# Modulation weights in 1 MB tiles, tokens by feature, and norms from a product with ones, in a hybrid decoder step

## The chip, the cores and the metric

The kernel runs on one core of one Trainium2 chip. Its engines are TensorE (PE; its weight loads are shown as PEld), VectorE (DVE), ScalarE (ACT), GpSimd (POOL) and SyncE (SP); 16 DMA engines move data between HBM and SBUF. The metric is the device time of one execution in microseconds, taken as the median of several runs. A profile is one further execution, recorded by the hardware profiler.

## What is computed

One decoder layer for 512 prompt tokens and 32 sampled tokens (8 sequences of 4), with 1024 features. Cut to what matters here:

```python
def ada_modulation(c, w_ada, b_ada):                  # w_ada: (1024, 6 * 1024)
    mod = (jax.nn.silu(c) @ w_ada + b_ada).reshape(c.shape[0], 6, 1024)
    return [mod[:, None, i] for i in range(6)]

def rms_norm(x, gain):
    return x * lax.rsqrt(jnp.mean(x * x, axis=-1, keepdims=True) + EPS) * gain

def decoder_layer(x, c, ...):
    sh_m, sc_m, gt_m, sh_f, sc_f, gt_f = ada_modulation(c, w_ada, b_ada)
    h = rms_norm(x, g_norm_mix) * (1 + sc_m) + sh_m
    u, q, k, v, g_a, g_b = jnp.split(h @ w_in, cuts, axis=-1)
    a = pool_mixer(u, ...) @ w_branch_pool
    o = attend(q, k, v) @ w_branch_attn               # prompt: causal; sampled: 3 best of 16 cached blocks
    x = x + gt_m * ((sigmoid(g_a) * a + sigmoid(g_b) * o) @ w_out)
    h2 = rms_norm(x, g_norm_ffn) * (1 + sc_f) + sh_f
    f_gate, f_val = jnp.split(h2 @ w_up, 2, axis=-1)
    return x + gt_f * ((silu(causal_dwconv(f_gate)) * f_val) @ w_down)
```

There are 9 condition vectors c: one for the prompt, eight for the sampled sequences. The sampled tokens read paged caches of K and V, 64 MB each as they are gathered here.

## The kernel before

**Work and stages.** All 544 tokens (512 and 32) go through the dense layers together. A weight piece of 128 x 1024 floats (a granule, 0.5 MB) is split into a high and a low part (`split`), and each product is three fp32r products (`mm3`). The stages are: h from x, then q, k and v, the prompt's attention with u between, the gates, the branches, w_out, up and down. Beside this dense stream runs the sampled stream: it gathers K in 64 tiles of 1 MB (`kstep`), chooses blocks, gathers V in 64 tiles, and multiplies the other modulation columns. A planner in the kernel deals the two streams out on TensorE by a running estimate of TensorE's time (`PE.now`) and of when a tile has landed. From there each engine works its queue off in order.

**The start.** `load_constants` (L282) loads x by token, two tiles of 256 tokens and one of 32 (`xin`). `norms` (L513) squares and sums each token's row on ScalarE, forms 1/sqrt(mean + eps) for each token, and spreads the 544 values over all partitions as rows (`rows`) by products with the identity. `turned` turns one feature block of 128 to 128 x 512 with four transposes on TensorE, `normed` multiplies it by the rows.

`quarter(i)` (L549) does two of the eight feature blocks: it multiplies the conditions by the shift and scale columns of these blocks, in two tiles of w_ada (kind `m0`, eight in all), turns and adds the bias (`modT`), forms the gain (`gsm`), and makes h for the sampled (`put_sample_h`) and the prompt's tokens (`put_prompt_h`) in high and low parts. The q projection follows the quarters: granule g of q takes h of quarter g, and quarter g + 1 is dealt out between its products. A `pair` or `st` tile holds a q granule; the sampled tokens' q is a product of the raw tile with `h1s`.

**What sets the order around the change.** SP's queue holds, in the program's order: cT, the constants, x, the `m0` tiles with one or two granules between, the page table (`ptb`), then granules, constants and gains. A transfer there waits for what its memory held before, and all behind it wait too. The tiles `m0` with numbers 2 to 4 have memory of their own (`m`), which `ptb` later uses again; so `ptb` waits until TensorE has read the fifth of them. `page_indices` (L299) makes the row numbers on VectorE, behind the third quarter's work there, and the first gather of K on GpSimd's queue waits for them. Each `m0` tile is loaded by two transfers, one for the shift and one for the scale columns, in runs of 256 floats (1 KB); the tiles of the other columns come in runs of 8 KB (`mod`) or 4 KB (`one`).

Of the kernel before, what the change touches and what calls it, by code (L numbers as in the profile page):

```python
# [74 lines left out]
def body(ctx, tc, I, O):  # L75
# [198 lines left out]
    xin = [consts.tile([128, 2, D], F32, name=uid("xin")) for _ in range(2)] + [consts.tile([NS, D], F32, name="xsin")]  # L274
# [7 lines left out]
    def load_constants():  # L282
        in_order(nc.sync.dma_start(cst[:, 0:CFIRST], I["const"][:, 0:CFIRST]))
        for i in range(2):
            in_order(nc.sync.dma_start(xin[i], I["x"][i * 256:(i + 1) * 256].rearrange("(t p) d -> p t d", p=128)))
        in_order(nc.sync.dma_start(xin[2], I["x"][S:T]))
# [31 lines left out]
    class Stream:  # L318
# [7 lines left out]
        def pump(self):  # L326
            while self.issued < len(self.items) and self.issued < self.at + NKV:
# [16 lines left out]
                elif kind == "m0":  # L344
                    rows = I["w_ada"][a[1] * 512:(a[1] + 1) * 512].rearrange("(k p) c -> p k c", p=128)
                    for v in range(2):
                        c0 = v * D + a[0] * 256
                        in_order(nc.sync.dma_start(kt.rearrange("p (k v c) -> p k v c", k=4, v=2)[:, :, v], rows[:, :, c0:c0 + 256]))
# [9 lines left out]
                elif kind == "mod":  # L358
                    pin(nc.gpsimd.dma_start(kt, I["w_ada"][a[1] * 128:(a[1] + 1) * 128, a[0] * 2048:(a[0] + 1) * 2048]))
                elif kind == "one":  # L360
                    pin(nc.gpsimd.dma_start(kt.rearrange("p (k c) -> p k c", k=2),
                                            I["w_ada"][a[1] * 256:(a[1] + 1) * 256, a[0] * D:(a[0] + 1) * D].rearrange("(k p) c -> p k c", p=128)))
                else:
                    pin(nc.gpsimd.dma_start(kt.rearrange("p (g c) -> p g c", g=2), I["wpack"][a:a + 2].rearrange("g p c -> p g c")))
# [139 lines left out]
    def dense1():  # L504
        hh, hl = [slot([128, T], F32R) for _ in range(8)], [slot([128, T], F32R) for _ in range(8)]
        ssx = consts.tile([128, 8], F32, name="ssx")
# [6 lines left out]
        def norms():  # L513

            rstd = consts.tile([128, 8], F32, name="rstd")
            for t in range(5):
                n, xt = (128, xin[t // 2][:, t % 2]) if t < 4 else (NS, xin[2])
                junk = wsh.next()
                act(junk[:n], xt[:n], AF.Square, accum_out=ssx[:n, t:t + 1])
                if t % 2 == 1 or t == 4:  # L520
                    c = slice(t // 2 * 2, t + 1)
                    V.tensor_scalar(rstd[:n, c], ssx[:n, c], 1.0 / D, EPS, op0=OP.mult, op1=OP.add)
                    act(rstd[:n, c], rstd[:n, c], AF.Sqrt)
                    V.reciprocal(rstd[:n, c], rstd[:n, c])
# [3 lines left out]
            PE.matmul(prs, rstd[:NS, 4:5].to_broadcast([NS, 128]), ident[:NS, :NS], start=True, stop=True)  # L528
            act(rows[:, 0:S], pr)
            act(rows[:, S:T], prs)  # L530

        def normed_sampled():
            prs = mm([128, 8, NS], "hT")
            for f in range(8):
                PE.transpose(prs[:, f], xin[2][:, f * 128:(f + 1) * 128], ident[:NS, :NS])
            return prs
# [1001 lines left out]
```

## Time and profile before

| what | value |
|---|---|
| time, median of 3 runs | 1002.61 us (1002.35 to 1004.32) |
| the profiled execution: time, span | 1004.91 us, 1003.0 us |
| TensorE busy | 955.2 us, 95% of the span |
| VectorE, ScalarE, GpSimd busy | 46%, 33%, 14% |
| moved by DMA | 236.62 MB |
| mean granted clock of TensorE | 0.98 |

How to read it: busy shares are means over stages with different limits, so a stage is looked at by itself, in a stretch of the timeline. Timeline rows merge equal instructions that follow each other: start, duration of the whole row, the instruction with out<-in by the program's names, a count, and in brackets the idle time before it and what ended it. An fp32 product shows as two records, an fp32r product as one. L163 and L167 are the lines of the helpers through which all products and transposes go, so tile names tell them apart: `hT` transposes and spread rows, `mod` modulation, `qkv` the projections, `qk` the cached K.

### The profile page before, as it was taken

How to read it: one execution, taken by the hardware profiler on the slowest of the kernel's cores; microseconds unless marked ns; L12 is line 12 of the kernel's file. 1: busy time of each engine (PE TensorE's matmuls, PEld its weight loads, DVE VectorE, ACT ScalarE, POOL GpSimd, SP SyncE). 2: the span in 40 equal slices, each digit the busy share in tenths (PEclk: the TensorE clock that was granted, in tenths of full speed). 3: DMA queues.
4: the chain of work that ended last, by engine and by line, in shares of the span. 5: the costliest groups of instructions: out<-in, count | busy, mean ns of one | idle time of the engine just before them, and what ended most of it. 6: DMA issues, size and time to landing. Idle time of an engine off the chain costs nothing.

```text
span 1003.0 us, 20225 instructions
## 1 busy us (share of the span) xinstructions
PE 955.2 (95%) x8674; PEld 809.6 (81%) x8674; DVE 465.9 (46%) x1071; ACT 328.8 (33%) x662; POOL 143.9 (14%) x157
## 2 busy tenths in 40 slices
PE   5979997999989999999999979999999999999998
PEld 3557775655579987777686779999989999999997
DVE  2572444656643332212384486554423545445455
ACT  5251425523422244111232354322233323123320
POOL 0043232133333332232200000000000000000000
PEclk9998999899999999999999989999999999999999
DMA  9799999499999996999956303222322222222222
GB/s 303 256 383 420 416 403 415 161 423 412 387 374 391 412 390 256 422 417 420 406 192 250 109 25 106 85 85 86 98 71 85 85 84 90 97 89 93 85 85 68
DMA packets 56266, 236.62 MB, mean 236 GB/s; under 512 B 5361, under 2 KB 17553, under 8 KB 38769
## 3 DMA queue, kind: packets, MB, share of 16 engines
q0 software_dynamic: 22848, 155.20, 38.1%
q1 hardware_dynamic: 33328, 80.13, 23.5%
q8 instruction: 68, 1.11, 0.4%
q14 instruction: 22, 0.17, 0.1%
HBM read 230.37 MB, written 4.94 MB: 235 GB/s over the span
## 4 chain that ended last, share of the span: by engine, by line
PE 86%; DMA 5%; ACT 4%; DVE 3%; issue 1%; POOL 0%; SPq 0%; DVEq 0%; ACTq 0%
PE up L163 26%; PE dn L163 13%; PE gate L163 10%; PE qkv L163 7%; PE pv L163 5%; PE qk L163 5%; PE wo L163 4%; PE mod L163 3%; PE O L163 2%; PE A L163 2%; DMA kv<-in_kT,kidx 2%; ACT spots L183 2%; ACT s L183 1%; DMA kv<-in_v,vidx 1%; PE u L163 1%; DVE s L180 1%
## 5 line engine op out<-in xcount | busy, mean ns | idle before, releaser
L180 DVE TENSOR_TENSOR lo<-st,hi 128x1024 fp32r<-128x1024 f32 x108 | 132.2, 1224 | 249.0 <-ACT hi L183 245.4
L163 PE MATMUL up<-s,hi 128*128 128x272 f32 x1408 | 234.6, 288 | 0.1
L183 ACT ACTIVATE hi<-st 128x1024 fp32r<-128x1024 f32 x108 | 114.4, 1059 | 342.1 <-PE up L163 115.5
L163 PEld LDWEIGHTS up<-s,hi 128*128 128x128 f32 x1408 | 199.1, 188 | 0.4 <-ACT hi L183 0.4
L163 PE MATMUL up<-s,lo 128*128 128x272 f32 x704 | 146.3, 288 | 0.5 <-DVE lo L180 0.5
L163 PE MATMUL dn<-s,hi 128*128 128x272 f32 x704 | 117.7, 289 | 0.0
L163 PEld LDWEIGHTS up<-s,lo 128*128 128x128 f32 x704 | 111.1, 188 | 0.7 <-DVE lo L180 0.7
L163 PEld LDWEIGHTS dn<-s,hi 128*128 128x128 f32 x704 | 98.9, 188 | 3.4 <-issue 2.5
L338 POOL DMA_INDIRECT kv<-in_kT,kidx x64 | 65.8, 1028 | 169.0 <-PE qk L163 104.7
L163 PE MATMUL gate<-s,hi 128*128 128x272 f32 x512 | 89.7, 296 | 0.0
L342 POOL DMA_INDIRECT kv<-in_v,vidx x64 | 63.7, 995 | 147.8 <-PE pv L163 116.7
L163 PEld LDWEIGHTS gate<-s,hi 128*128 128x128 f32 x512 | 72.5, 189 | 11.5 <-issue 10.4
L183 ACT ACTIVATE s<-s 128x544 f32<-128x544 f32 (+4 forms) x74 | 46.7, 644 | 81.1 <-DVE s L1269 37.5
L163 PE MATMUL dn<-s,lo 128*128 128x272 f32 x352 | 72.8, 288 | 0.0
L163 PE MATMUL qkv<-hi,s 128*128 128x512 f32 x192 | 70.2, 421 | 2.3 <-ACT s L183 2.0
L163 PE MATMUL qk<-kv,qblk 128*32 128x128 f32 x2048 | 65.2, 277 | 6.1 <-DVE qblk L632 1.9
L163 PEld LDWEIGHTS qk<-kv,qblk 128*32 128x32 f32 x2048 | 55.1, 111 | 15.0 <-issue 8.9
L163 PE MATMUL pv<-kv,spots 128*32 128x512 f32 x512 | 63.3, 605 | 0.4 <-DMA kv<-in_v,vidx 0.4
L180 DVE TENSOR_TENSOR s<-s,s 128x544 fp32r<-128x544 f32 (+4 forms) x78 | 53.6, 700 | 14.0 <-ACT s L183 13.6
L163 PEld LDWEIGHTS qkv<-hi,s 128*128 128x128 f32 x192 | 37.0, 193 | 23.0 <-issue 12.2
L163 PEld LDWEIGHTS dn<-s,lo 128*128 128x128 f32 x352 | 55.2, 188 | 0.0
L163 PE MATMUL gate<-s,lo 128*128 128x272 f32 x256 | 53.0, 288 | 0.0
(217 smaller groups left out, 1183.7 us busy)
## 6 DMA issues: line engine op xcount, KB each, us to landing
st<-in_wpack SPq DMA_DIRECT2D x108, 512.0 KB, 3.4
kv<-in_w_ada POOLq DMA_DIRECT2D x16, 1024.0 KB
kv<-in_w_ada SPq DMA_DIRECT2D x10, 512.0 KB, 10.9
kv<-in_wpack POOLq DMA_DIRECT2D x4, 1024.0 KB
pair<-in_wpack SPq DMA_DIRECT2D x6, 512.0 KB, 14.2
m<-in_w_ada SPq DMA_DIRECT2D x6, 512.0 KB, 4.7
xin<-in_x SPq DMA_DIRECT2D x2, 1024.0 KB, 7.5
s<-in_x SPq DMA_DIRECT2D x8, 256.0 KB, 6.4
```

The lines of the kernel that those rows point to most:

```text
L163: return self.add(nc.tensor.matmul(out, lhsT, rhs, **kw))
L180: V.tensor_tensor(out, a, b, op)
L183: A.activation(out, x, func, **kw)
L338: pin(nc.gpsimd.indirect_dma_start(out=kt, out_offset=None, in_=krows, in_offset=bass.IndirectOffsetOnAxis(ap=kidx[:, i:i + 1], axis=0)))
L342: pin(nc.gpsimd.indirect_dma_start(out=kt, out_offset=None, in_=vrows, in_offset=bass.IndirectOffsetOnAxis(ap=vidx[:, i:i + 1], axis=0)))
```

## The change

Three layouts change, made from the inputs before the kernel starts. The modulation weights come as 24 tiles of 128 x 2048 floats, each contiguous, 8 KB for a partition; every tile is one transfer. x comes a second time by feature, as four tiles of 128 x (2 x 544) (`xT`); x by token is still read later for the residual. The transposes of x, `turned` and `normed_sampled`, go away. The norms are found from x by feature: each block is squared on ScalarE, two squares are added on VectorE, and a product with ones sums over the 128 features of a block into every partition, for both halves of the tokens; mean, eps, square root and reciprocal then run on 128 x 272 instead of one column a token block. The products of one `m0` tile are bound into a run (`PE.begin`, `PE.end`).

```diff
+    xT = consts.tile([128, KD, T], F32, name="xT")
+    ones = consts.tile([128, 1], F32, name="ones")
+    V.memset(ones, 1.0)
...
-        for i in range(2):
-            in_order(nc.sync.dma_start(xin[i], I["x"][i * 256:(i + 1) * 256].rearrange("(t p) d -> p t d", p=128)))
-        in_order(nc.sync.dma_start(xin[2], I["x"][S:T]))
+        for i in range(4):
+            in_order(nc.sync.dma_start(xT[:, 2 * i:2 * i + 2], I["xT"][i].rearrange("p (f c) -> p f c", f=2)))
...
                 elif kind == "m0":
-                    rows = I["w_ada"][a[1] * 512:(a[1] + 1) * 512].rearrange("(k p) c -> p k c", p=128)
-                    for v in range(2):
-                        c0 = v * D + a[0] * 256
-                        in_order(nc.sync.dma_start(kt.rearrange("p (k v c) -> p k v c", k=4, v=2)[:, :, v], rows[:, :, c0:c0 + 256]))
+                    in_order(nc.sync.dma_start(kt, I["wada"][j]))
...
                 elif kind == "mod":
-                    pin(nc.gpsimd.dma_start(kt, I["w_ada"][a[1] * 128:(a[1] + 1) * 128, a[0] * 2048:(a[0] + 1) * 2048]))
+                    pin(nc.gpsimd.dma_start(kt, I["wada"][8 + a[1]]))
                 elif kind == "one":
-                    pin(nc.gpsimd.dma_start(kt.rearrange("p (k c) -> p k c", k=2),
-                                            I["w_ada"][a[1] * 256:(a[1] + 1) * 256, a[0] * D:(a[0] + 1) * D].rearrange("(k p) c -> p k c", p=128)))
+                    pin(nc.gpsimd.dma_start(kt, I["wada"][16 + 4 * (a[0] - 4) + a[1]]))
...
         def norms():
-            rstd = consts.tile([128, 8], F32, name="rstd")
-            for t in range(5):
-                n, xt = (128, xin[t // 2][:, t % 2]) if t < 4 else (NS, xin[2])
-                junk = wsh.next()
-                act(junk[:n], xt[:n], AF.Square, accum_out=ssx[:n, t:t + 1])
...
-            pr, prs = mm([128, S], "hT"), mm([128, NS], "hT")
-            for t in range(4):
-                PE.matmul(pr[:, t * 128:(t + 1) * 128], rstd[:, t:t + 1].to_broadcast([128, 128]), ident, start=True, stop=True)
...
+            pr = [mm([128, HALF], "hT") for _ in range(2)]
+            for i in range(4):
+                sq = [slot([128, T]) for _ in range(2)]
+                for j in range(2):
+                    act(sq[j], xT[:, 2 * i + j], AF.Square)
+                tt(sq[0], sq[0], sq[1], OP.add)
+                for o, (a, b) in zip(pr, BOTH):
+                    PE.matmul(o, ones.to_broadcast([128, 128]), sq[0][:, a:b], start=i == 0, stop=i == 3)
+            for o, (a, b) in zip(pr, BOTH):
+                V.tensor_scalar(rows[:, a:b], o, 1.0 / D, EPS, op0=OP.mult, op1=OP.add)
+                act(rows[:, a:b], rows[:, a:b], AF.Sqrt)
+                V.reciprocal(rows[:, a:b], rows[:, a:b])
...
-        def turned(f):
-            ps = mm([128, S], "hT")
-            for t in range(4):
-                PE.transpose(ps[:, t * 128:(t + 1) * 128], xin[t // 2][:, t % 2, f * 128:(f + 1) * 128], ident)
-            return ps
-        def normed(ps):
+        def normed(f):
             x = slot([128, S])
-            tt(x, ps, rows[:, 0:S], OP.mult)
+            tt(x, xT[:, f, 0:S], rows[:, 0:S], OP.mult)
             return x
...
             if i == 0:
-                raw = [turned(0), turned(1)]
-                prs = normed_sampled()
                 norms()
...
+            xT2 = [normed(f0), normed(f0 + 1)]
             ps = mm([128, 256], "mod")
             for a in range(2):
                 st = KV.get("m0").rearrange("p (k v c) -> p k v c", k=4, v=2)
+                PE.begin()
                 for kk in range(4):
                     for v in range(2):
                         j = 2 * (kk % 2) + v
                         PE.matmul(ps[32 * j:32 * j + 32], csT[:, 4 * a + kk], st[:, kk, v],
                                          start=a == 0 and kk < 2, stop=a == 1 and kk >= 2)
+                PE.end()
                 KV.next()
...
-            if i:
-                xT = [normed(turned(f0))]
...
+def pack_modulation(w):
+    w = w.reshape(KD, 128, 6, D)
+    tiles = [w[4 * h:4 * h + 4, :, 0:2, c * 256:(c + 1) * 256].transpose(1, 0, 2, 3) for c in range(4) for h in range(2)]
+    tiles += [w[k, :, 2:4] for k in range(KD)]
+    tiles += [w[2 * k:2 * k + 2, :, v].transpose(1, 0, 2) for v in (4, 5) for k in range(4)]
+    return np.stack([t.reshape(128, 2048) for t in tiles])
```

The change moves instructions at three places. The first is SP's queue from the first `m0` tile on. In brackets stand the semaphores a transfer waits for: `DMAHW` names are those of earlier transfers on the queue, the others are engines. Before:

```order
L348 DMA kv<-in_w_ada 128x4x256 [waits DMAHW1_49]
L220 DMA pair_100<-in_wpack 128x1024 [waits DMAHW2_49,PE_49,Pool_49]
L348 DMA m_102<-in_w_ada 128x4x256 [waits DMAHW3_49]
...
L348 DMA kv<-in_w_ada 128x4x256 [waits DMAHW3_49]
L220 DMA pair_112<-in_wpack 128x1024 [waits DMAHW4_49,DVE_49,PE_49]
L348 DMA kv<-in_w_ada 128x4x256 [waits DMAHW5_49]
...
L289 DMA ptb<-in_page_table 128x256 [waits DMAHW1_49,PE_49]
```

In the changed kernel, the same stretch of SP's queue:

```order
L347 DMA kv<-in_wada 128x2048 [waits DMAHW0_49]
L220 DMA pair_99<-in_wpack 128x1024 [waits DMAHW1_49]
L347 DMA m_101<-in_wada 128x2048 [waits DMAHW2_49]
...
L347 DMA kv<-in_wada 128x2048 [waits DMAHW6_49]
L220 DMA pair_107<-in_wpack 128x1024 [waits DVE_49,DMAHW7_49,PE_49,Activation_49]
L347 DMA kv<-in_wada 128x2048 [waits DMAHW0_49]
L347 DMA kv<-in_wada 128x2048 [waits DMAHW1_49]
L291 DMA ptb<-in_page_table 128x256 [waits DMAHW3_49,DMAHW5_49,DMAHW2_49,PE_49]
```

Eight `m0` transfers stand where sixteen stood. By the values they wait for, the first pair waited for the last product that spreads the norms, and now waits for no engine. The second waited for the first pair to be split and multiplied by `h1s`; it now waits for TensorE's last product with ones and for earlier work of VectorE and ScalarE. The page table still waits for the product that reads the fifth `m0` tile.

The second place is VectorE's queue from the norms to the first gain; `s` are working tiles, `xsT` the normed sampled tokens. Before:

```order
L522 TENSOR_SCALAR rstd<-ssx 128x2
L522 TENSOR_SCALAR rstd<-ssx 32x1
L524 RECIPROCAL rstd<-rstd 128x2
L524 RECIPROCAL rstd<-rstd 32x1
L180 TENSOR_TENSOR s_181<-hT_136,s_133 128x512
L180 TENSOR_TENSOR xsT<-hT_146,s_133 128x256
L180 TENSOR_TENSOR s_183<-hT_141,s_133 128x512
L180 TENSOR_TENSOR modT<-mod_224,par 128x2x18
L581 SCALAR_TENSOR_TENSOR gsm<-modT,par 128x18
```

In the changed kernel:

```order
L180 TENSOR_TENSOR s_153<-s_153,s_154 128x544
L521 TENSOR_SCALAR s_127<-hT_130 128x272
L521 TENSOR_SCALAR s_127<-hT_131 128x272
L523 RECIPROCAL s_127<-s_127 128x272 x2
L180 TENSOR_TENSOR xsT<-xT,s_127 128x256
L180 TENSOR_TENSOR s_168<-xT,s_127 128x512
L180 TENSOR_TENSOR s_170<-xT,s_127 128x512
L180 TENSOR_TENSOR modT<-mod_209,par 128x2x18
L560 SCALAR_TENSOR_TENSOR gsm<-modT,par 128x18
```

The bias of the first quarter (`modT`) stands behind two reciprocals of 272 columns instead of three of one or two columns.

The third place is TensorE's queue at the second quarter, between the first q products; `m` is the tile of modulation weights. Before:

```order
L163 MATMUL qkv_243<-hi,s_114 128x512
L163 MATMUL mod_253<-m_102,csT 32x256
L163 MATMUL qkv_243<-lo,s_114 128x512
L163 MATMUL qkv_244<-hi,s_114 128x512
L163 MATMUL qkv_244<-lo,s_114 128x512
L163 MATMUL mod_253<-m_102,csT 32x256 x7
...
L163 MATMUL mod_253<-m_102,csT 32x256
L167 MATMUL hT_280<-cst,xin_84 128x128 x2
L167 MATMUL hT_280<-cst,xin_85 128x128 x2
L163 MATMUL qkv_246<-hi,s_114 128x512
```

In the changed kernel:

```order
L163 MATMUL qkv_228<-hi,s_109 128x512
L163 MATMUL qkv_228<-lo,s_109 128x512
L163 MATMUL mod_242<-m_101,csT 32x256 x8
L163 MATMUL qkv_229<-hi,s_109 128x512
L163 MATMUL qkv_229<-lo,s_109 128x512
L163 MATMUL qkv_228<-hi,s_117 128x512
L163 MATMUL qkv_229<-hi,s_117 128x512
L163 MATMUL mod_242<-m_101,csT 32x256 x8
```

The transposes of x are gone, and the eight products of a tile stand together. Of the six tiles dealt out among the q products, four stood divided before; two do now (the fifth tile, one and seven, and the seventh, five and three).

## Rows read from the trace of the kernel before

**Rows 1.** The page: the span, and TensorE's and the DMA engines' busy tenths in 40 slices.
```profile
span 1003.0 us, 20225 instructions
...
PE   5979997999989999999999979999999999999998
...
DMA  9799999499999996999956303222322222222222
```

**Rows 2.** Stretches: us, each engine's busy us (instructions), granted clock, DMA share, GB/s.
```profile
6.00:8.00 2.00, 1.09 (x4) 0.71 (x4) 0.00 (x0) 1.26 (x3) 0.00 (x0) 1.00 1.03 424
20.00:30.00 10.00, 8.87 (x38) 4.18 (x40) 4.19 (x9) 1.76 (x4) 0.00 (x0) 0.66 1.09 360
34.00:36.00 2.00, 2.00 (x13) 0.75 (x12) 2.00 (x6) 0.29 (x1) 0.00 (x0) 1.00 0.00 0
70.00:90.00 20.00, 16.40 (x229) 11.75 (x223) 9.64 (x20) 3.29 (x7) 8.10 (x7) 0.83 1.02 418
```

**Rows 3.** Timeline of TensorE, 0 to 64 us: start, duration, instruction, idle before.
```profile
9.71 1.11 PE L167 MATMUL hT<-cst,xin 128*128 128x128 f32 x4 [1.76 <-DMA xin<-in_x]
...
15.04 2.93 PE L163 MATMUL mod<-kv,csT 128*32 128x256 f32 x32
...
21.13 0.80 PE L163 MATMUL qkv<-hi,s 128*128 128x512 f32 x1 [1.99 <-ACT s L183]
...
36.43 0.62 PE L163 MATMUL mod<-m,csT 128*32 128x256 f32 x2
36.98 0.50 PE L163 MATMUL qkv<-hi,s 128*128 128x512 f32 x1
...
41.84 0.60 PE L167 MATMUL hT<-cst,xin 128*128 128x128 f32 x4
42.20 0.47 PE L163 MATMUL qkv<-hi,s 128*128 128x512 f32 x1
...
47.21 1.07 PE L163 MATMUL mod<-kv,csT 128*32 128x256 f32 x16
...
63.59 0.40 PE L163 MATMUL qkv<-hi,s 128*128 128x512 f32 x1
```

**Rows 4.** Timeline of SP's queue, 15 to 40 us: when transfers are issued.
```profile
15.19 0.34 SPq L220 DMA_DIRECT2D pair<-in_wpack  x1
...
35.87 0.34 SPq L220 DMA_DIRECT2D pair<-in_wpack  x1
...
38.52 1.21 SPq L289 DMA_DIRECT2D ptb<-in_page_table  x1
```

**Rows 5.** Timeline of GpSimd, 50 to 52 us: the first gather of K.
```profile
50.70 2.17 POOL L338 DMA_INDIRECT kv<-in_kT,kidx  x1 [48.20 <-DVE vidx L312]
```

**Rows 6.** Timeline of TensorE, 62 to 88 us: the first K tiles.
```profile
66.80 4.12 PE L163 MATMUL qk<-kv,qblk 128*32 128x128 f32 x119 [1.93 <-DVE qblk L632]
71.22 0.50 PE L163 MATMUL qk<-kv,qblk 128*32 128x128 f32 x9 [0.31 <-issue]
73.60 1.08 PE L163 MATMUL qk<-kv,qblk 128*32 128x128 f32 x32 [1.89 <-ACT spots L183]
76.09 1.94 PE L163 MATMUL qk<-kv,qblk 128*32 128x128 f32 x32 [1.41 <-DMA kv<-in_kT,kidx]
...
84.38 1.95 PE L163 MATMUL qk<-kv,qblk 128*32 128x128 f32 x64
```

**Rows 7.** Groups by line and shape: out<-in, shape, count, busy us, mean ns, idle before.
```profile
L183 ACT ACTIVATE s<-s 128x544 f32<-128x544 f32 x22 | 14.5, 658 | 62.2 <-DVE s L1269 37.5 <-DVE s L501 24.8
...
L180 DVE TENSOR_TENSOR s<-s,s 128x544 f32<-128x544 f32 x8 | 5.8, 719 | 0.0
...
L163 PE MATMUL pg<-s,s 128*128 128x272 f32 x16 | 5.5, 475 | 3.1 <-DVE s L180 3.0 <-ACT s L183 0.2
...
L770 DVE RECIPROCAL st<-st 128x1 f32<-128x1 f32 x32 | 5.1, 161 | 4.1 <-ACT s L183 3.2
...
L449 DVE RECIPROCAL st<-st 128x8 f32<-128x8 f32 x8 | 1.6, 195 | 0.0
```

More of the change, by code (lines that the diff above doesn't have):

```diff
@@ L272, in body @@
     ptb = consts.tile([128, 256], I32, name="ptb")
-    xin = [consts.tile([128, 2, D], F32, name=uid("xin")) for _ in range(2)] + [consts.tile([NS, D], F32, name="xsin")]
+    xT = consts.tile([128, KD, T], F32, name="xT")
+    ones = consts.tile([128, 1], F32, name="ones")
+    V.memset(ones, 1.0)
     pin = tc.keep_in_program_order
@@ L505, in dense1 @@
         hh, hl = [slot([128, T], F32R) for _ in range(8)], [slot([128, T], F32R) for _ in range(8)]
-        ssx = consts.tile([128, 8], F32, name="ssx")
         gsm = consts.tile([128, 8, 9], F32, name="gsm")
@@ L513, in norms @@
         def norms():
-            rstd = consts.tile([128, 8], F32, name="rstd")
-            for t in range(5):
-                n, xt = (128, xin[t // 2][:, t % 2]) if t < 4 else (NS, xin[2])
-                junk = wsh.next()
-                act(junk[:n], xt[:n], AF.Square, accum_out=ssx[:n, t:t + 1])
[L520 to L524, printed above, removed]
-            pr, prs = mm([128, S], "hT"), mm([128, NS], "hT")
-            for t in range(4):
-                PE.matmul(pr[:, t * 128:(t + 1) * 128], rstd[:, t:t + 1].to_broadcast([128, 128]), ident, start=True, stop=True)
[L528 to L536, printed above, removed]
-        def turned(f):
-            ps = mm([128, S], "hT")
-            for t in range(4):
-                PE.transpose(ps[:, t * 128:(t + 1) * 128], xin[t // 2][:, t % 2, f * 128:(f + 1) * 128], ident)
-            return ps
-        def normed(ps):
+            pr = [mm([128, HALF], "hT") for _ in range(2)]
[11 more added lines that the diff above has]
+        def normed(f):
             x = slot([128, S])
-            tt(x, ps, rows[:, 0:S], OP.mult)
+            tt(x, xT[:, f, 0:S], rows[:, 0:S], OP.mult)
             return x
@@ L552, in quarter @@
             if i == 0:
-                raw = [turned(0), turned(1)]
-                prs = normed_sampled()
                 norms()
                 xsT = consts.tile([128, 8, NS], F32, name="xsT")
-                tt(xsT, prs, rows[:, None, S:T].to_broadcast([128, 8, NS]), OP.mult)
+                tt(xsT, xT[:, :, S:T], rows[:, None, S:T].to_broadcast([128, 8, NS]), OP.mult)
                 state["xsT"] = xsT
-                xT = [normed(r) for r in raw]
+            xT2 = [normed(f0), normed(f0 + 1)]
             ps = mm([128, 256], "mod")
@@ L583, in quarter @@
             put_sample_h(hh, hl, state["xsT"][:, fs], gsm, shm, fs, h1s)
-            put_prompt_h(hh, hl, f0, xT[0], gsm, shm)
+            put_prompt_h(hh, hl, f0, xT2[0], gsm, shm)
             yield 0.3
-            if i:
-                xT.append(normed(turned(f0 + 1)))
-            put_prompt_h(hh, hl, f0 + 1, xT[1], gsm, shm)
+            put_prompt_h(hh, hl, f0 + 1, xT2[1], gsm, shm)
             yield 0.3
@@ L1496 @@
     a = {k: np.asarray(v) for k, v in inputs.items()}
+    x_all = np.concatenate([a["x_prompt"][0], a["x_sample"].reshape(NS, D)], axis=0)
     c_all = np.concatenate([a["c_prompt"], a["c_sample"]], axis=0)
@@ L1503 @@
     feed = {
-        "x": np.concatenate([a["x_prompt"][0], a["x_sample"].reshape(NS, D)], axis=0),
+        "x": x_all,
         "cT": c_all.reshape(9, KD, 128).transpose(2, 1, 0),
-        "w_ada": a["w_ada"][0],
+        "xT": x_all.T.reshape(4, 2, 128, T).transpose(0, 2, 1, 3).reshape(4, 128, 2 * T),
+        "wada": pack_modulation(a["w_ada"][0]),
         "b_ada": a["b_ada"],
```

## Prediction

> **What bounds the kernel now.** I read the slices of the span first. TensorE is nearly full in every slice except a few, and the weak ones lie at the start and around 62 to 82 us [rows 1]; the DMA engines are busy at 0.9 and more until about 480 us and then fall back. So the end is set by the row of TensorE work, and a change at the start is worth what it moves that row forward, if nothing later gives it back.
>
> The second view is TensorE's own timeline up to 64 us. It starts transposes when the second half of x has landed (9.71), works off the sums of the first modulation columns at 15.04, and begins the q projection at 21.13. From there it hardly stops until the last q product, which starts at 63.59 and ends at 63.99 [rows 3]. So the q stage, 42.9 us long, is bound by TensorE itself: by the products, by the modulation products put between them, by the transposes of x, and by a clock whose mean from 20 to 30 us is 0.66, between its levels of 0.50 and 1.00 (1.2 and 2.4 GHz) [rows 2].
>
> The third view is SP's queue. One pair of weights is issued only at 15.19, the next at 35.87, and the page table at 38.52 [rows 4]. In 34 to 36 us the DMA engines move nothing at all [rows 2]. The page table gates the gather of K pages, whose first instruction had waited until 50.70 [rows 5]. The fourth view is TensorE at the first K tiles: it starts them at 66.80, waits 1.89 us for ScalarE to clear the bank after four tiles, and 1.41 us for the sixth tile's DMA at 76.09. That tile takes 1.94 us, where later two tiles take 1.95 [rows 6]: the clock is low again there, 0.83 in the mean of 70 to 90 us [rows 2].
>
> **The order after the start does not change.** From the first K product to the end, TensorE's instructions stand in the same order in both kernels, apart from names; so do the transfers. All that the change can do directly lies before 67 us, and the rest is moved as a block.
>
> **1. The start, to the first q product: 1.3 us won (bounds 2.5 won, 1.7 lost).** x by feature has the same 2.23 MB and the same place in the queue, so its last quarter lands where the second half of x did, at about 9.7 us [rows 3]. Behind it: two squares of 0.66, one sum of 0.72 [rows 7], two products with ones, 1.1 together (475 ns for a record of this shape), then, scaled by width from the rows of 544, mean and epsilon 0.4, square root 0.4, two reciprocals over 272 columns, the sampled rows (0.4) and two normed blocks (0.7 each). The reciprocals are not in the trace at this width: 1 column takes 161 ns, 8 take 195 [rows 7], which is 4.9 ns for each further column. At that slope one of 272 columns takes 1.5 us, both 3.0. If the slope were an effect of small sizes, they would cost 0.2 each; at twice the slope, 3 us each. I take 3.0 for both. The chain then ends at 18.5 us; bias and gain follow on the same engine and the scaled block on ScalarE, 1.3 of the 3.2 us that lie before between the end of the modulation products (17.97) and q, and q starts at 19.8 instead of 21.13. The cheap end is bounded by the weights: the second 1 MB tile lands 2.2 MB after x, at the 424 GB/s of 6 to 8 us [rows 2] at 15.0, its products take 1.1, and then 2.5 us as before between their end and the first q product: 18.6. The dear end is 22.8.
>
> The Trainium skill, "VectorE: DVE Perf Modes", section "First, the fixed hardware budget", says that the reciprocal is an iterative divide with a repeat count of 8. Estimated from that page as eight cycles a column, both reciprocals would take 4.6 us instead of 3.0, q would start at 21.4, and the whole sum would come to 7.3 us won. The row with 8 columns speaks for the smaller slope, but no row has this width.
>
> **2. The q stage: 3.6 us won.** Of the transposes, the first two sets lie before the q stage; six sets of four go from inside it. One set moves the next q product by 0.36 us (41.84 to 42.20) [rows 3]: 2.2 us. Second, the modulation products of one tile now form a run. Before, four of the six tiles inside the stage had one product ahead and seven behind a q product; such an early piece costs 0.55 us (36.43 to 36.98), and the seven behind it save next to nothing against an undivided tile, which takes 1.07 [rows 3]. The new order still divides two. Two pieces fewer, one of them at half clock (0.85): 1.4 us. VectorE's multiplies read x from SBUF instead of PSUM, and they lie beside TensorE's work: nothing. The other 16 modulation tiles keep their size and place; they are prefetched behind V, under TensorE's work: nothing, and if uncovered, a change in their rate moves only the few of them that TensorE would wait for. The eight products with ones take the place of transposes before the stage and are in part 1. So the last q product ends at 63.99 - 1.3 - 3.6 = 59.1.
>
> **3. The page table and the K tiles: 3.0 us won.** The first pair no longer waits for the broadcast of the norms, and the second no longer waits for the first to be used; the transfers run on through the gap at 34 us. The last modulation tile lands 10.0 MB after x, at 424 GB/s at 33 us, well before TensorE wants it. The page table still waits for the fifth modulation tile to be read, and the indices stand behind the third quarter on VectorE. Ahead of that lie the 1.3 us of part 1, three of the six transpose sets (1.1) and three of the four pieces (2.0). So the gather starts 4.4 us earlier, at 46.3.
>
> From 43 us the queues then hold 2.1 MB of gains and weights, six K tiles of 1.05 MB and up to 1.0 MB of weights. At the rate of the saturated stretch from 70 to 90 us, 418 GB/s [rows 2], the sixth tile lands at 65 to 66. TensorE starts K at 59.1 + 2.8 = 61.9 and asks for that tile 7.9 us later (66.80 to the end of the fifth, 74.68) [rows 6], at 69.8. The wait of 1.41 is gone. The sixth tile then need not run at half clock (1.0). The first four took 4.9 us for 128 records, where 64 later take 1.95 [rows 6], so 1.0 us too long, of which I take 0.6. The bank's 1.89 stays. If all of this stays, nothing is won (0); if all goes, 3.4.
>
> **4. The clock: 1.0 us won (bounds 5 won, 3 lost).** A mean of 0.66 over 10 us is 6.8 us at the lower level, one of 0.83 over 20 us again 6.8 [rows 2]. Half of each is lost: 3.4 and 3.4, of which 1.0 is already counted. Both follow pauses of TensorE, which shrink but don't vanish. I take one more microsecond at the second place and nothing at the first.
>
> **The sum.** 1.3 + 3.6 + 3.0 + 1.0 = 8.9 us. The profiled execution took 1004.91 with a span of 1003.0 [rows 1], so its span would be 994.1 and its time 996.0. It stands 2.3 us above the median of the runs, 1002.61; against that the forecast is 993.7.
>
> **Rivals.**
> - *The DMA takes over (chance 0.17).* From 60 to 170 us the engines are full at about 420 GB/s. If they set the pace there, TensorE only gets what the transfers gained, and waits for K tiles from the seventh on. For it: the DMA row is full there [rows 1]. Against it: TensorE is full as well from 80 us on, and the transfers are ahead by more than TensorE is, the sixth tile by 10 us. If it holds, parts 3 and 4 are lost: 4.9 us won, 997.7.
> - *The clock stays up (0.16).* With six fewer pauses in the order and the first wait shorter, both stretches at half speed vanish. 4 to 5 us more than the sum: 989.
> - *Nothing to measure (0.08).* The reciprocals at their dear end take 3 us back, and the transfers take over: 1001.5.
> - *TensorE at half clock through the q stage (0.06).* The eight products with ones are sparse where transposes and row products were dense, so TensorE comes into the q stage after a longer lull. A stretch at the lower level costs half its length; from 24.6 us on (6.8 plus twice 8.9) it takes all that is won, and if it lasted the whole q stage, 39 us, the kernel would take 993.7 + 16 = 1010. Against it: in the kernel before the lower level lasted 6.8 us there and ended while q ran on.
>
> **How the numbers follow.** My own case has the remaining 0.53; its range is 990.5 to 997 (the bounds of part 1, and part 3 from 1 to 3.4). Reaching to the two neighbours gives 987 to 1000.5, which leaves out the last two rivals and some of the clock's. A difference under 0.2%, 2 us, can't be told from none: faster 0.86, same 0.08, slower 0.06.
>
> **What would show it.** The first q product near 19.8 us; reciprocals of 272 columns at about 1.5 us; the end of the q products near 59; no gap in the transfers at 34 us; the first K gather near 46; no wait for a K tile at TensorE before 80; and from there every mark (first V products, wo, up, dn) earlier by about 9 us. The forecast is wrong if TensorE waits for K tiles after the sixth, if q starts later than 21, or if the gain at 85 us isn't found again at 580.

## The result and the profile after

The changed kernel takes 993.29 us (median of 4 runs, 991.06 to 995.53) against 1002.81 for the kernel before on the same chip (4 runs). The ratio is 0.9895, 95% interval 0.9874 to 0.9915: 9.5 us won, where 8.9 were forecast. A second set of runs beside the experiments gave 0.9912 (0.9891 to 0.9933). The profiled execution took 993.18 with a span of 991.4.

The page after, answering to [rows 1]: span, TensorE and the DMA engines in 40 slices.

```profile
span 991.4 us, 20154 instructions
...
PE   4989997899989999999999889999999999999998
...
DMA  9799999499999997999955313222222332223322
```

The stretches after, answering to [rows 2] (us, busy us of each engine with instructions, granted clock, DMA share, GB/s).

```profile
20.00:30.00 10.00, 8.69 (x52) 5.06 (x53) 6.62 (x16) 3.20 (x6) 0.00 (x0) 0.69 1.02 417
34.00:36.00 2.00, 2.00 (x18) 0.83 (x17) 2.00 (x3) 0.00 (x0) 0.00 (x0) 1.00 0.03 8
62.00:68.00 6.00, 4.69 (x112) 4.51 (x116) 5.37 (x17) 4.73 (x15) 2.00 (x2) 0.72 1.03 420
70.00:90.00 20.00, 20.00 (x311) 15.93 (x301) 7.82 (x15) 4.52 (x8) 8.97 (x9) 1.00 1.01 419
```

Transfers in 20 to 30 us rose from 360 to 417 GB/s, but the gap at 34 us, which was to go, is still there. TensorE is no longer idle in 70 to 90 us. The second stretch at the lower clock now falls on the first K tiles, at 62 to 68.

TensorE's timeline after, answering to [rows 3] and [rows 6].

```profile
8.13 6.07 PE L163 MATMUL hT<-s,ones 128*128 128x272 f32 x16 [8.13 <-DVE pidf L307]
14.13 1.07 PE L163 MATMUL mod<-kv,csT 128*32 128x256 f32 x16
15.44 1.07 PE L163 MATMUL mod<-kv,csT 128*32 128x256 f32 x16 [0.23 <-DMA kv<-in_wada]
17.01 0.66 PE L163 MATMUL mod<-cst,s 128*128 128x64 f32 x4 [0.50 <-ACT s L183]
21.31 0.80 PE L163 MATMUL qkv<-hi,s 128*128 128x512 f32 x1 [3.64 <-ACT s L183]
...
60.26 0.40 PE L163 MATMUL qkv<-hi,s 128*128 128x512 f32 x1
60.59 0.43 PE L167 MATMUL qkT<-cst,s 32*128 32x32 f32 x4
63.31 5.38 PE L163 MATMUL qk<-kv,qblk 128*32 128x128 f32 x128 [2.28 <-ACT qblk L609]
69.41 1.96 PE L163 MATMUL qk<-kv,qblk 128*32 128x128 f32 x64 [0.72 <-ACT spots L183]
71.18 0.60 PE L163 MATMUL qkv<-pair,h1s 128*32 128x512 f32 x2
```

The modulation sum is done at 17.67, then TensorE waits 3.64 us; q starts 0.2 us *later* than before. The last q product ends 3.3 us earlier (60.66 for 63.99), and the wait for a K tile is gone. VectorE's timeline shows what TensorE waits for at the start.

```profile
11.44 0.72 DVE L180 TENSOR_TENSOR s<-s,s 128x544 f32<-128x544 f32 x1 [0.60 <-ACT s L183]
13.78 0.90 DVE L521 TENSOR_SCALAR s<-hT 128x272 f32<-128x272 f32 x2 [1.62 <-PE hT L163]
14.78 3.56 DVE L523 RECIPROCAL s<-s 128x272 f32<-128x272 f32 x2
18.38 0.42 DVE L180 TENSOR_TENSOR xsT<-xT,s 128x256 f32<-128x256 f32 x1
18.72 1.29 DVE L180 TENSOR_TENSOR s<-xT,s 128x512 f32<-128x512 f32 x2
19.93 0.19 DVE L180 TENSOR_TENSOR modT<-mod,par 128x36 f32<-128x36 f32 x1
...
39.75 0.20 DVE L180 TENSOR_TENSOR modT<-mod,par 128x36 f32<-128x36 f32 x1 [3.55 <-PE mod L163]
...
43.58 0.24 DVE L311 TENSOR_SCALAR kidx<-ptb,pidf 32x64 int32<-32x64 int32 x1
```

The bias (modT) needs only the sum of 17.67, but it stands behind two reciprocals and three multiplications until 19.93. Before, the same two rows of the third quarter, its bias and the first indices, stood at:

```profile
44.22 0.19 DVE L180 TENSOR_TENSOR modT<-mod,par 128x36 f32<-128x36 f32 x1
...
48.83 0.24 DVE L309 TENSOR_SCALAR kidx<-ptb,pidf 32x64 int32<-32x64 int32 x1
```

SP issues the page table at 35.88 (38.52 in [rows 4]). It has stood before that load since 17.0, until the fifth `m0` tile was read, and so the gap at 34 us stays. GpSimd starts the first K gather 5.25 us earlier than in [rows 5]. SP's row and GpSimd's:

```profile
35.88 0.33 SPq L291 DMA_DIRECT2D ptb<-in_page_table  x1
```

```profile
45.45 2.17 POOL L340 DMA_INDIRECT kv<-in_kT,kidx  x1 [42.96 <-DMA s<-in_g_q]
```

Where the time went, by starts on TensorE's timeline (us; `q ends` and the last column are ends). `Sampled k` is the first product of the sampled tokens' k, `paS` the scores of the prompt's attention; gate, wo and up are the first products of the gates, w_out and up. e5 is the changed kernel in a second trace, the others are experiments below.

| | first q | q ends | sampled k | first paS | gate | wo | up | end |
|---|---|---|---|---|---|---|---|---|
| before | 21.13 | 63.99 | 77.80 | 164.46 | 292.01 | 524.04 | 588.41 | 998.78 |
| after | 21.31 | 60.66 | 71.18 | 155.99 | 281.88 | 512.61 | 577.32 | 987.16 |
| e5 | 21.73 | 61.42 | 72.05 | 156.85 | 281.99 | 512.64 | 577.92 | 987.72 |
| e9 | 20.30 | 59.43 | 74.64 | 160.01 | 284.82 | 516.67 | 581.94 | 991.76 |
| e10 | 20.26 | 59.21 | 69.77 | 154.59 | 281.38 | 513.05 | 578.30 | 988.01 |
| e11 | 22.20 | 59.79 | 69.48 | 154.88 | 278.91 | 510.36 | 572.67 | 983.46 |

From before to after: -0.2 at q's start, 3.5 in the q stage, 3.3 from there to the products of the sampled k (behind the first six K tiles), 1.9 up to the first paS: 8.5 us by 156 us. That gain is kept, and the pair of traces shows 3 us more by the end. The traced execution of the kernel before is itself 2.1 us above the median of its runs, so most of this may be chance. A window of the clock does not explain it: from 376 to 384 us the kernel before ran at a granted 0.79, the changed kernel at 1.00 in the same work (366 to 374) and e5 at 0.79, and yet after and e5 take 230.7 us each from gate to wo.

### The profile page after: what moved, and what is told of

It is laid out like the page before. It is cut to its first block, busy times and chain, and to the rows that moved or that the text cites. A ratio compares the mean times of both kernels' runs of the same rounds, so it can differ in the third digit from the quotient of the medians.

```text
span 991.4 us, 20154 instructions
## 1 busy us (share of the span) xinstructions
PE 946.1 (95%) x8640; PEld 803.8 (81%) x8640; DVE 472.0 (48%) x1074; ACT 327.6 (33%) x657; POOL 142.2 (14%) x157
## 4 chain that ended last, share of the span: by engine, by line
PE 86%; ACT 5%; DVE 3%; DMA 3%; issue 2%; SPq 0%; POOL 0%; DVEq 0%; ACTq 0%
PE up L163 26%; PE dn L163 13%; PE gate L163 10%; PE qkv L163 8%; PE qk L163 6%; PE pv L163 5%; PE wo L163 4%; PE O L163 2%; PE mod L163 2%; ACT s L183 2%; PE A L163 2%; ACT spots L183 2%; DMA kv<-in_v,vidx 1%; PE u L163 1%; DVE s L180 1%
## 5 line engine op out<-in xcount | busy, mean ns | idle before, releaser
L183 ACT ACTIVATE s<-s 128x544 f32<-128x544 f32 (+5 forms) x76 | 47.6, 638 | 82.5 <-DVE s L1246 37.4
L180 DVE TENSOR_TENSOR s<-s,s 128x544 fp32r<-128x544 f32 (+4 forms) x82 | 56.3, 701 | 21.5 <-ACT s L183 21.2
## 6 DMA issues: line engine op xcount, KB each, us to landing
m<-in_wada SPq DMA_DIRECT2D x3, 1024.0 KB, 14.2
```

Source lines behind the costliest of these rows:

```text
L180: V.tensor_tensor(out, a, b, op)
L183: A.activation(out, x, func, **kw)
```

## The experiments

**e1 and e2: each part alone.** e1 is the kernel before with the 1 MB tiles, e2 the changed kernel with the old loads.

```diff
# e1, on the kernel before
-  two transfers of w_ada for each tile: rows[:, :, c0:c0 + 256]
+  in_order(nc.sync.dma_start(kt, I["wada"][j]))
# e2, on the changed kernel: the same lines the other way round
```

> The kernel before with one part of the change alone: the modulation weights come as 1 MB tiles in one transfer each; x is still handed over by token and turned by transposes. Theory A (the gain is mostly the removed transposes and, on SP, the earlier index table): the first q product stays at 21.1 us within 0.4, because the path through rstd and the transposes still sets it; the q stage keeps its 36 us or so; transfers from 10 to 30 us go up from about 340 to about 420 GB/s; the whole is 0 to 3 us faster than before, 1000 to 1003 us. Rival B (the transfers were the bound): most of the 9.5 us comes from here, 994 to 996 us, with the first q product at 20 us or earlier.

> The changed kernel with the modulation weights loaded as before (two transfers of 1 KB runs for each tile): x by feature and the norms by a product with ones alone. Theory A: most of the gain is here, 994 to 997 us; the last q product ends 2 to 3 us earlier than in the kernel before (61 to 62 us), the first K gather stands 3 us or more earlier than 50.7. Rival B (the transfers were the bound): 1000 to 1003 us, the first q product waits for a modulation tile rather than for ScalarE. If the two parts add up, the gains of this run and of the layout alone together make 9.5 us.

Measured: e1 0.9961 (0.9941 to 0.9982), e2 0.9935 (0.9912 to 0.9957). In us of the kernel before that is 3.9 and 6.5, together 10.4 against 9.5: within the noise the parts add up, neither is the whole, and rival B falls. Two forecasts were missed: in e1 the transfers of 10 to 30 us did not reach 420 GB/s (355, for 338 before), and in e2 the last q product ended at 63.30, not at 61 to 62. So the missing transposes alone do not tell how long the q stage is. The windows of the q stage, from the first to the end of the last q product, of e1, e2 and the changed kernel:

```profile
20.65:61.74 41.09, 41.08 (x246) 24.79 (x246) 25.11 (x60) 14.47 (x28) 7.84 (x6) 0.96 0.83 308
```

```profile
21.25:63.30 42.05, 41.28 (x223) 22.99 (x224) 25.03 (x61) 14.57 (x28) 6.12 (x6) 0.94 0.88 313
```

```profile
21.31:60.66 39.35, 39.17 (x223) 23.03 (x224) 25.00 (x61) 14.58 (x28) 7.90 (x6) 0.94 0.85 331
```

With the transposes gone, e2's stage is longer than e1's, which has them. The second batch of the sampled tokens' q takes 3.8 us of TensorE's line in e2 (51.95 to 56.31, less 0.6 of other work, with 0.77 of wait for VectorE), and 1.0 us in e1. e10 takes this up.

**e3: the page table at the start.**

```diff
     load_constants()
+    load_pages()
+    page_indices()
     KV = Stream()
```

> The kernel before with one edit: the page table is loaded and its indices are worked out at the start, so that SP does not stand before that load until 38.5 us and the K gathers can start without it. Theory A (part 3 of the prediction: the K tiles' landing is worth 3 us): the first K gather starts before 46 us instead of 50.7, the waits of TensorE for K tiles (1.4 us in all) go, the fall to half clock at 75 us goes or moves, and the whole is 2 to 4 us faster than before, 999 to 1001 us. Rival B: something else (the head-norm chain that makes the block of q, or the falling clock) takes the place of the K wait: within 1 us of before. Rival C: the gathers, now early, take the transfers' time from the weights that q needs, and it is slower than before.

Measured: 1.0006 (0.9988 to 1.0025). The first gather starts at 13.38 us. Theory A and rival C both hold and cancel: TensorE waits 2.7 us for a modulation tile and q's first product starts at 23.57, so the first K product comes 6.0 us later than before; from there to the first u product it takes 102.81 us instead of 107.06, 4.3 won. Early K tiles are worth something, but not if they take the transfers that q needs.

**e4: narrow reciprocals.**

```diff
-  PE.matmul(o, ones.to_broadcast([128, 128]), sq[0][:, a:b], start=i == 0, stop=i == 3)
+  PE.matmul(pn[:n, i, t:t + 1], sq[0][:, t * 128:t * 128 + n], ones, start=True, stop=True)
+  ... sum of four, mean, root and reciprocal over 4 columns and 1, spread by five products
```

> The changed kernel with the sums taken per token (the squares as the stationary operand and one column of ones), so that the reciprocals run over 4 columns and 1 column instead of twice 272, and five products spread the result. Theory A (the step that failed in the prediction is the price of the two wide reciprocals, 3.56 us on VectorE, behind which stand the normed blocks and the modulation sum): VectorE starts the normed blocks at 16.5 to 17.2 instead of 18.4 us, the first q product starts at 19.5 to 20.2 instead of 21.3, and the whole is 1 to 2 us faster than the changed kernel, 991 to 992.5 us. [...] Rival C (the modulation tiles or the first weight pair set the start, whatever the norms do): the first q product stays within 0.3 of 21.3, 993 us.

Measured: 0.9945 (0.9927 to 0.9963), slower than the changed kernel; q starts at 25.49. The reciprocals shrank to 0.24 us, but TensorE paid. Its timeline:

```profile
7.75 8.02 PE L163 MATMUL hT<-ones,s 128*128 128x1 f32 x40 [7.75 <-DVE pidf L307]
16.69 2.63 PE L163 MATMUL hT<-cst,rstd 128*128 128x128 f32 x10 [0.92 <-DVE rstd L526]
19.25 3.64 PE L163 MATMUL mod<-kv,csT 128*32 128x256 f32 x32
```

The sums are 20 products of one moving column (40 records), 0.40 us each, and the spreading products stand ahead of the modulation products. A miss for every theory: the cost moved to the other engine.

**e5: the changed kernel again.** No edit; it stands beside e6 to e8.

> The changed kernel once more, beside the next three on one chip, so that they can be compared with it. Ratio to the kernel before 0.9895 as measured (0.9874 to 0.9915); its first q product at 21.3 and the end of the first K tiles' block as in its first trace.

Measured: 0.9912 (0.9891 to 0.9933), 994.91 us. Its marks are in the table: q starts at 21.73, 0.4 us later than in the first trace.

**e6: the first wait filled.**

```diff
+  for _ in range(7):
+      PE.matmul(hot, ones.to_broadcast([128, 128]), xT[:, 0, 0:HALF], start=True, stop=True)
   fs = slice(f0, f0 + 2)
```

> The changed kernel with seven products of 128x272 with ones on TensorE, whose result nobody reads, between the modulation sum of the first quarter (ends at 17.7 us) and the first q product (21.3): 3.3 us of work in a wait of 3.6. Theory A (the clock falls because TensorE pauses there): the stretch at 1.2 GHz from 19.3 to 27 us goes; the q stage ends 2.5 to 3.5 us earlier (57.2 to 58.2 instead of 60.66), and the whole is 2 to 3.5 us faster than the changed kernel. Rival B (the clock falls anyway, for what TensorE did earlier): the stretch stays, the time is the same within 1 us, or up to 0.5 longer if the seven products end after the scaled block is there. Rival C (the gain is given back at the first K product, because the head norms or the gathers hold it): the q stage ends 3 us earlier, but the first block of K waits longer and nothing is left at 90 us.

Measured: 0.9903 (0.9878 to 0.9929), not to be told from e5. The clock did what theory A says, granted 1.00 from 17 to 30 us, but the q stage took 38.98 us, hardly less than 39.35, since TensorE at full clock meets the next wait:

```profile
17.14 3.43 PE L163 MATMUL mod<-xT,ones 128*128 128x272 f32 x14
20.97 0.49 PE L163 MATMUL qkv<-hi,s 128*128 128x512 f32 x1 [0.40 <-ACT s L183]
...
23.70 0.49 PE L163 MATMUL qkv<-hi,s 128*128 128x512 f32 x1 [1.20 <-DVE s L180]
```

VectorE's chain to the low halves sets the pace there. The stretch at 1.2 GHz was mostly cover for that wait.

**e7: VectorE's order at the start.** The second normed block and the sampled rows are written after the gain.

> The changed kernel with VectorE's order at the start changed: after the two reciprocals only the first normed block is made, then the modulation sum and the gain; the second normed block comes after them. Theory A (VectorE's queue behind the wide reciprocals sets the start): modT starts at 19.2 to 19.4 instead of 19.93, the first q product at 20.4 to 20.8 instead of 21.31, 0.5 to 0.9 us won there; the first block of the next feature comes no later than TensorE wants it, and the whole is 0.5 to 1 us faster than the changed kernel. Rival B: the second half of the first features is now late and TensorE waits between the first q products, nothing won or up to 0.5 us lost.

Measured: 0.9918 (0.9899 to 0.9938), as e5. modT started at 18.77 and q at 20.08, but TensorE then waited 0.47 us for VectorE, one more modulation tile was divided, and q ended at 60.89. Rival B.

**e8 and e9: the K gather held back.** In e8 six casts on GpSimd write a tile of their own, in e9 the tile that the first gather then fills.

```diff
   if kind == "k":
+      if i == 0:
+          for _ in range(6):
+              pin(nc.gpsimd.tensor_copy(junk, kidx[:, 0:32, None].to_broadcast([128, 32, 16])))   # e9: kt[:, 0:512]
```

> The changed kernel with the first K gather held back: six useless casts of 128x512 on GpSimd stand between the K indices and the first gather, an estimated 3 to 6 us, so that the gather starts at 48.5 to 51.5 us, about where it stood in the kernel before (50.70), while everything else stays. Theory A (part 3: the landing of the first K tiles is worth 3 us): TensorE waits again for the fifth to seventh K tile, and it is 1.5 to 3.5 us slower than the changed kernel. Rival B (the K tiles wait for the block of q and for the bank anyway): the same as the changed kernel within 1 us.

Measured: 0.9993 (0.998 to 1.0007), but not as a test: the added tile changed VectorE's order, so that the indices came ahead of the second quarter's bias and waited there for the page table; the gather started at 41.18, earlier, and TensorE waited 4.3 us for VectorE inside the q stage. It shows only that the indices' place in VectorE's queue matters.

> The changed kernel with the first K gather held back again, this time with no other engine's order touched: the six casts (4.22 us together in the run before this) write into the tile that the first gather then fills. The first gather should start near 49.7 us instead of 45.45, about where the kernel before had it (50.70), with the q stage as it is. Theory A (part 3 of the prediction: that the first K tiles land early is worth about 3 us): TensorE waits for K tiles between 65 and 80 us, the mark at the first V products is 1.5 to 3.5 us later than in the changed kernel, and so is the end. Rival B (the block of q and the bank hold TensorE anyway): the marks after 80 us stay within 0.7 us.

Measured: 0.9954 (0.9936 to 0.9971), 4 to 6 us slower than the changed kernel. The gather, and TensorE at the K tiles:

```profile
49.83 1.15 POOL L343 DMA_INDIRECT kv<-in_kT,kidx  x1 [0.29 <-POOL kv L342]
```

```profile
62.08 5.57 PE L163 MATMUL qk<-kv,qblk 128*32 128x128 f32 x128 [2.28 <-ACT qblk L612]
70.53 1.08 PE L163 MATMUL qk<-kv,qblk 128*32 128x128 f32 x32 [2.89 <-ACT st L183]
72.93 1.93 PE L163 MATMUL qk<-kv,qblk 128*32 128x128 f32 x32 [1.32 <-DMA kv<-in_kT,kidx]
```

Here q ends 1.2 us earlier than in the changed kernel and the sampled k comes 3.5 later: 4.7 us for a gather 4.4 us late, and the end is 4.6 later. That is the pattern of [rows 6]. The row of 70.53 names ScalarE, but the bank had been cleared by 68.31; the last piece of the fifth tile landed within 0.2 us of 70.53. Part 3's mechanism stands; rival B falls.

**e10: the six transpose sets back as dead work.**

```diff
+  if i:
+      turned(f0)          # four transposes of xT into PSUM, read by nobody
   put_prompt_h(hh, hl, f0, xT2[0], gsm, shm)
   (the same for f0 + 1)
```

> The changed kernel with the six transpose sets of the q stage put back as work that nobody reads (24 transposes of 128x128 at the places where they stood); the norms still come from the products with ones. In this order no modulation tile is divided, where the changed kernel divides two. Theory A (part 2: 0.36 us of TensorE for each set, some 0.5 for each dividing): the q stage takes 2.2 us more for the transposes and up to 1.0 less for the two pieces, so 40.5 to 41.6 us instead of 39.35 to 39.7, and the whole is 1 to 2.2 us slower than the changed kernel. Rival B (VectorE's chain for the quarters sets the q stage, as the run with a full clock suggests, so TensorE has room): the q stage stays within 0.5 us of 39.5.

Measured: 0.9895 (0.9875 to 0.9914), no slower than the changed kernel. The q stage, and the transposes in it (shape, count, busy us, mean ns):

```profile
20.26:59.21 38.95, 38.95 (x246) 24.74 (x246) 24.80 (x61) 14.64 (x28) 7.31 (x6) 0.95 0.87 342
```

```profile
L167 PE MATMUL hT<-cst,xT 128*128 128x128 f32 x24 | 3.5, 273 | 0.0
```

TensorE is busy for the whole 38.95 us, so rival B's reason (room on TensorE) is wrong though its number came out. This order divides no modulation tile. Length times granted clock, to take the clock out, is 37.0 here and in the changed kernel. Yet the transposes are not free: from the start of each set to the next product, the six sets take 2.2 us together in e10, as theory A has it. Two things in the changed kernel's order cost as much. Its two divided tiles take 1.53 us each at full clock (one from 42.95 to 43.92 and 44.35 to 44.91), an undivided one 1.00. And the second batch of the sampled tokens' q takes 2.04 us (with 0.18 of wait), in e10 0.99. The changed kernel:

```profile
51.64 1.05 PE L163 MATMUL qkv<-pair,h1s 128*32 128x512 f32 x4
52.45 1.05 PE L163 MATMUL qkv<-st,h1s 128*32 128x512 f32 x4
53.68 0.50 PE L163 MATMUL qkv<-hi,s 128*128 128x512 f32 x1 [0.18 <-ACT s L183]
```

The same batch in e10:

```profile
51.19 0.62 PE L163 MATMUL qkv<-pair,h1s 128*32 128x512 f32 x2
51.20 0.62 PE L163 MATMUL qkv<-st,h1s 128*32 128x512 f32 x2
51.64 0.60 PE L163 MATMUL qkv<-pair,h1s 128*32 128x512 f32 x2
51.65 0.60 PE L163 MATMUL qkv<-st,h1s 128*32 128x512 f32 x2
52.18 0.50 PE L163 MATMUL qkv<-hi,s 128*128 128x512 f32 x1
```

Where the products of the two weight tiles take turns (e10, e1, before), they overlap and the batch takes 1.0 us; where one tile's stand ahead of the other's, it takes 2.0. Neither the prediction nor theory A had this price. The kernel before (39.9) has e10's transposes, its fast batches and four divided tiles, 2.1 us by the price above; 0.8 us of its distance to e10 stays open.

**e11: four waits filled.** As e6, and products that nobody reads before the first K product, before u (158 us) and before the second norm's transposes (566 us).

```diff
+  hot(5, "qkT")     # 128x224, after the transposes of the sampled q
+  one product of 128x128 and five of 128x512 behind the last K tiles ahead of u
+  hot(14, "h2T")    # 128x224
```

> The changed kernel with products that nobody reads in four waits of TensorE: seven of 128x272 before the first q product, five of 128x224 before the first K product (wait 2.28 us), five of 128x512 before the pool products u at 158 us (wait 7.07), fourteen of 128x224 before the transposes of the second norm at 566 us (wait 5.98). Theory A (half clock after a pause is lost time on the path): the stretches at 1.2 GHz near 20, 64, 166 and 572 us go, which are 3.3, 1.9, 3.4 and 3.4 us of lost time in the changed kernel's windows; the first is nearly worthless as the run with the first wait filled showed (1 us), so 5 to 8 us faster than the changed kernel, 986 to 989. Rival B (the other engines' chains, slower than TensorE at full clock there, take it back): at most 2 us.

Measured: 0.9858 (0.9838 to 0.9878), 989.92 us, the best of all and ahead of both kernels: 14.2 us less than before (0.0142 x 1002.8), 3.7 to 5.4 less than the changed kernel by its two sets of runs. Windows of e11:

```profile
18.00:22.00 4.00, 4.00 (x13) 3.07 (x12) 3.64 (x11) 1.77 (x4) 0.00 (x0) 0.64 1.02 421
162.00:170.00 8.00, 5.66 (x37) 4.80 (x38) 4.91 (x20) 5.06 (x17) 0.00 (x0) 0.79 1.00 384
566.00:578.00 12.00, 11.11 (x79) 9.81 (x79) 11.19 (x27) 9.08 (x24) 0.00 (x0) 1.00 0.15 46
```

At 566 to 578 the changed kernel had 0.72, at 162 to 170 it had 0.57. Up to the sampled k e11 stands 1.7 us ahead, at up 4.7. Theory A's 5 to 8 us are reached at its lower end at best, rival B's 2 us are passed. In 18 to 22 and 162 to 170 us the clock is not at full speed, so not all four stretches went.

**e12: no tile divided.** e11 without its start, each run of modulation products held behind the product issued before it.

```diff
-  PE.begin()
+  PE.begin(i > 0)     # the run's first product waits for the last one issued
```

> The kernel of the run before without its seven products at the start (their wait was worth about 1 us at most), and with each run of eight modulation products held behind the product that was issued before it, so that no modulation tile of the q stage is divided; the changed kernel divides two, the run with the dead transposes none. Theory A (each dividing costs TensorE about 0.7 us: the q stage, less the half of its time at 1.2 GHz, was 39.74 us in the kernel before with four divided tiles and 24 transposes, 36.91 with the 24 transposes and none divided, 36.93 in the changed kernel with two divided and no transposes): the q stage, reckoned in that way, comes to 35.3 to 35.8 us, its end to 58.0 to 59.5 us with the first q product at 20.3 to 21.7, and the whole to 1 us less than the run before, 988 to 989.5. Rival B (a product held behind another makes TensorE wait for ScalarE or VectorE instead): the q stage stays at 36.9 or grows, and the whole is as in the run before or up to 1 us slower.

Measured: 0.99 (0.9877 to 0.9923), 993.21 us. The stage is 40.07 us at a granted 0.90, times each other 36.1: above theory A's 35.8 and below rival B's 36.9. It has 1.7 us of waits for VectorE in it, which is rival B's reason; the whole is some 4 us slower than e11 by the ratios, more than rival B said. The products at the start are gone as well, so the two causes are not told apart. TensorE's waits from 17 to 62 us (in all, how often, the longest; the first is the one ahead of q):

```profile
PE qkv L164 <- ACT s L184: 3.4, 1, 3.4
PE qkv L164 <- DVE s L181: 1.7, 2, 1.5
```

What undivided tiles save TensorE goes here, by these numbers, into waits for VectorE.

## Why the prediction was right, and where not

The time and the chief mechanism were right, TensorE's row moved forward as a block: the sum said 8.9 us, the marks show 8.5 by 156 us, and the runs 9.5. All four rivals fell. That the total is so near is in part luck: 1.5 us missing at the start were made up by 0.3 at the K tiles and 0.9 behind them. Of the signs that it named, three failed: q came later than 21 us (21.31), its last product ended at 60.66 instead of near 59, and the gap at 34 us stayed. By steps:

- **Part 1, the start: wrong.** 1.3 us won were forecast, 0.2 lost came. The failed term is the chain from the squares to the rows. The last sum came 0.4 us later than reckoned (12.16 for 11.75), VectorE had the first product with ones 1.6 us behind it instead of 1.1 (TensorE worked on them without a pause from 8.13 to 14.20), the mean and root took 0.2 more, and the reciprocals 3.56 instead of 3.0: 1.78 us for 272 columns, 6.5 ns a column where [rows 7] gave 4.9 at small sizes. From the repeat count of 8 that the Trainium skill, "VectorE: DVE Perf Modes", section "First, the fixed hardware budget", states, the estimate was 4.6 for both; the 3.56 of the trace lie between. Over the five traces with this same start (after, e5, e8, e9, e10) q began at 20.26 to 21.73 us, with the same 3.56 us of reciprocals; the eight products with ones took 5.57 us in e10, 6.07 after and 6.88 in e5, at a granted 1.00 in all three. Why is open. e4 and e7 show that shortening or passing this chain hands the wait to another, and none of e4, e6 and e7 was worth more than a microsecond.
- **Part 2, the q stage: 3.5 won for 3.6, with one price missing.** The prices of its sum hold: 2.2 us for the six sets of transposes (e10), and the early pieces of divided tiles, 0.5 us each at full clock and 1.0 at half (21.85 to 22.84 before), come to 1.6 net where 1.4 was forecast. Missing was the second batch of the sampled q, 1.0 us lost to the new order. The rest, 0.7, lies in the clock (lost at the lower level, by length and granted clock: 3.0 us before, 2.4 after) and in what is not assigned.
- **Part 3, the K tiles: 3.3 won for 3.0.** The gather came 5.25 us earlier instead of 4.4, though the 1.3 of part 1 in that 4.4 did not come: the third bias came 4.5 us earlier, and the indices 3.8 us behind it instead of 4.6. e9, which takes the gather back alone, takes 4.7 back. The reason given holds: before and after, the indices stand on VectorE behind the third quarter's work. The wait for the sixth tile is gone (1.4), and the tile no longer runs at half clock (1.0). The rest came by other ways: the bank's wait, which was to stay at 1.89, fell to 0.72, and the first four tiles, which were to win 0.6, took 0.5 longer. Why the bank's wait fell is not shown. The gap at 34 us stayed; TensorE waited for no transfer behind it.
- **Part 4, the clock: 1.9 won for 1.0.** The stretch of lower clock moved from behind the K tiles (74 to 82 us at 0.57, the row below) into them (62 to 68 at 0.72). That the clock does not stay up by itself was right, and the rival that priced it at 4 to 5 us asked too much: filled, the first stretch gives about 1 us at most (e6, within the noise), since VectorE is next.

The kernel before, from 74 to 82 us:

```profile
74.00:82.00 8.00, 6.59 (x74) 4.05 (x63) 4.76 (x10) 0.21 (x1) 3.36 (x3) 0.57 1.02 419
```

## What to carry to other kernels

Price a removed instruction by what the engine does in the order that results: here the removed transposes were worth their 2.2 us, but the order that came of it gave 1.0 back in another batch, and the kernel with the transposes put back as dead work was no slower. Read from the queue, not from the data, when a step can start: the bias had its sum at 17.67 and stood behind VectorE's other work until 19.93, and the page table landed 4.4 us after its issue at 35.88, but the indices came at 43.58. A stretch at the lower clock is worth half its length only if the engine that feeds TensorE could go faster; fill the wait ahead of it and look for the next wait before counting on it.

## What was not expected of the hardware

- A wide reciprocal on VectorE: 1.78 us for 128x272, four times the 0.45 us of a mean and epsilon over the same block.
- A product of one moving column with 128 stationary ones: 0.40 us each (20 in 8.02 us, four of them with 32; e4), where the eight of 128x272 with ones took 6.07 in all.
- The transfers of one core: 417 GB/s in 20 to 30 us with runs of 4 and 8 KB, 360 with runs of 1 KB among them at a *higher* busy share (1.09 against 1.02).
- Two kinds of small products on TensorE: 1.0 us for a batch of the sampled q whose two weight tiles take turns (e10), 1.9 of work for the same batch one tile after the other.
- VectorE beside GpSimd: two multiplications of 128x512 took 1.64 us while GpSimd's casts ran (e8), 1.00 otherwise.
- The granted clock can differ for the same kernel and the same wait: 1.00 after and 0.79 in e5 behind 1.46 us of idle TensorE at 366 us; in e11 it fell at 18 us though TensorE had products to do from 17.45 on.
